# A hybrid decoder layer on one core: a third place for turned tiles in w_up, their steps in line there, and w_down's groups of seven at other steps

## The chip, the core and the metric

The kernel runs on one core of a Trainium2 chip. The time is that of one execution in device microseconds; smaller is better. A core has TensorE (PE, with a weight load PEld ahead of each matmul), VectorE (DVE), ScalarE (ACT), GpSimd (POOL) and SyncE (SP). Here SP issues nearly all loads of weights and the transposing DMAs, and POOL issues DMAs that add two weight blocks.

## The reference

One layer on 256 tokens of 2048 features in float32:

```python
u = rmsnorm(h, norm_mix_pre)
h = h + rmsnorm(hybrid_mixer(u, ...) , norm_mix_post)      # w_in, SSD and attention heads, w_out
hdn = relu(rmsnorm(h, norm_mlp_pre) @ w_up)                # 2048 -> 8192
h = h + rmsnorm((hdn * hdn) @ w_down, norm_mlp_post)       # 8192 -> 2048
```

The change touches the last two lines alone.

## The kernel before

**Exact products.** Matmuls are made of halves: every float32 operand is split into a high part (`hi`, a rounding copy on ACT, L150) and a low part (`lo`, the difference on DVE, L151), and a product is three matmuls, hi·hi, hi·lo and lo·hi (L382 to L384). A matmul of 128 x 128 by 512 columns is the unit in which TensorE's work is counted.

**Units.** `unit` (L502) computes a pair of column blocks of 512 for both token tiles of 128. It walks over `order`, steps of 256 rows of the weight (two blocks of 128). A plain step calls `row_tiles` for both column blocks: 24 matmuls, two loads of 512 KB, two splits of 128 x 1024. A step of the set `by_seven` calls `seven` (L437), which forms the same 2 x 2 x 2 block products from seven block products instead of eight: 21 matmuls. For that it needs sums of the activations' blocks (`sums_of_acts`, L419: four DVE additions and a split, made one step ahead and kept for the next unit) and sums of the weights' blocks: three additions on DVE (L275), and splits of `raw_a`, `e`, `raw_b` and `t4` (three of 128 x 1024, one of 128 x 512). One block of the second load is the sum of two blocks, which POOL forms in DRAM by two DMAs (`next_pair`, L293, up to four sevens ahead of its use); SP then loads it as the source `pair`. `combine_new` (L473) makes the accumulators' sums after a unit's last seven.

**Lookahead.** Split weights lie in five buffers of each kind (`BUFS`), raw weights in four and a few more that a stage has to spare (`room["raw"]`). ACT and DVE therefore run ahead of TensorE by little more than a step.

**The MLP.** w_up and w_down are taken in two halves (`hf`) of 4096 hidden features. In the first half w_up has three units (blocks 2 and 3, 4 and 5, 6 and 7), in the second half four. Each has seven steps in `order` with sevens at steps 1, 3, 4 and 6 (`UP_SEVENS`), and a last plain step of its own. Then w_down has two units in each half, for the columns 0 to 1023 and 1024 to 2047, with orders of 14 and 12 or 13 steps. The unit of columns 0 to 1023, here "the first w_down pair", is the one whose order changes.

**Turned tiles.** Each w_up unit leaves four tiles of 128 tokens x 512 hidden features in the queue `beside`. w_down needs them transposed. `turned` (L1517) does it in two parts. The first (the *pump*, `pump_beside`) is relu and square on ACT, a copy on ACT that sorts the 16-bit halves of the words into `halves`, and a transposing DMA on SP (L1525) back into the tile. The second (the *landing*, `land_beside`) is a copy on ACT that puts the 16-bit halves together, and the split into `sh` and `sl` or the like. `halves` is one of the places in `room["halves"]`: two in w_up, four in w_down of the first half, two in the second.

**When they stand.** `TURNS` and `LANDS` (L58, L59) name the steps at which `unit` pumps one tile and lands one; the first tuple of each is for orders of seven steps, the second for longer ones. A pump stands ahead of its step's weights, a landing behind them. w_up's tiles are pumped and landed in the next unit; those of a half's last w_up unit in the first w_down pair.

**Order on the engines.** A scheduler places instructions by priority, and what is at high priority keeps the program's order. `in_line` adds an order written out by hand: an instruction in it comes behind the last split or addition of the line on ACT and DVE (`line`). Weights' splits and additions are in line. A turned tile's copies and split are in line in w_down (`exact`), except for the landing at step 0; in w_up they have ordinary priority, only not before the newest split, and the scheduler places them between the others. In both cases relu and square have ordinary priority.

**Temporaries.** `tmp` gives tiles `r` (four buffers), and `sum_tile` gives `e` (one buffer). Both already look for tiles of their own in `room["own"]` and `room["sum"]`, which no function of the kernel before sets.

Of the kernel before, what the change touches and what calls it, by code (L numbers as in the profile page):

```python
# [10 lines left out]
F32 = mybir.dt.float32  # L11
F32R = mybir.dt.float32r
BF16 = mybir.dt.bfloat16
U16 = mybir.dt.uint16
AF = mybir.ActivationFunctionType
ALU = mybir.AluOpType

P = 128
# [21 lines left out]
NB = 512  # L40
KB = 2
# [13 lines left out]
V_SEVENS = (1, 3, 5, 6)  # L55
QK_SEVENS = (1, 3, 5, 6)
PAIRS_AHEAD = 4
TURNS = ((1, 2, 4, 5), (3, 4, 8, 9))  # L58
LANDS = ((0, 3, 4, 6), (0, 6, 7, 10, 11))  # L59


def constants():
# [18 lines left out]
def hymba_layer(ctx: ExitStack, tc: tile.TileContext, x, norm_mix_pre, w_in, conv_w, conv_b, dt_bias, a_log,  # L81
                d_skip, ssm_norm_w, w_out, norm_mix_post, norm_mlp_pre, w_up, w_down, norm_mlp_post,
                consts, out):
    nc = tc.nc
    w_in, w_out, w_up, w_down = w_in[0], w_out[0], w_up[0], w_down[0]
# [61 lines left out]
    def split(hi, lo, src, scale=None):  # L147

        if scale is None:
            return (nc.scalar.activation(hi, src, AF.Copy),  # L150
                    nc.vector.tensor_tensor(lo, src, hi.bitcast(F32), op=ALU.subtract))  # L151
        return (nc.scalar.activation(hi, src, AF.Copy, scale=scale),
                nc.vector.scalar_tensor_tensor(lo, src, scale, hi.bitcast(F32), op0=ALU.mult, op1=ALU.subtract))
# [27 lines left out]
    room = {}  # L181
# [13 lines left out]
    def beside_up(raws, turn, halves=None):  # L195

        room["sums"] = [v[:, k:k + KB] for k in range(0, NK // 2, KB) for v in att[1]]
        b = hp.tile([P, NT, NB], F32, name="hb")
        room["shared"] = [[b[:, t] for t in range(NT)],
                          [hp.tile([P, NB], F32, name="wpost", bufs=2) for _ in range(NT)]]  # L200
        room["last"] = deque([room["shared"][1].pop(), hp.tile([P, NB], F32, name="junk")])
        room["shared"][1].append(room["last"][0])
        a = hp.tile([P, 3 * KB, NB], F32, name="ha")
        in_a = [a[:, k:k + KB] for k in range(0, 3 * KB, KB)]
        halves = in_a.pop(0) if halves is None else halves
        room["halves"] = deque(halves[:, i].bitcast(U16) for i in range(KB))
        room["raw"], room["turn"], room["acts"], room["chain"] = [*raws, *in_a], turn, act_u, True
        room["of_halves"], room["of_a"] = halves, in_a
        sums_of.clear()

    def beside_down():

        a = hp.tile([P, 3 * KB, 2, S], F32R, name="ha")
        room["sums"] = [a[:, k] for k in range(3 * KB)]
        room["raw"], room["turn"], room["acts"] = [mws[2]], 0, part
        room["halves"] = deque(mws[0][:, t, c0:c0 + NB].bitcast(U16) for t in range(NT) for c0 in (0, NB))
        room["then"] = [(4, halves_beside_down), (2, more_beside_down), (0, all_beside_down)]
        sums_of.clear()
# [60 lines left out]
    w_z, w_v, w_ups, w_downs = w_in[:, COL_Z:], w_in[:, COL_V:], [w_up[:, hf * 4096:] for hf in range(2)], [w_down, w_down[4096:]]  # L279
# [8 lines left out]
    def plan(name, src, n, order, by_seven):  # L288

        orders[name, n] = order_of(order, by_seven)  # L290
        pairs.extend((src, blocks_of(n), k) for k in order if k in by_seven)
# [55 lines left out]

    beside, flying = deque(), deque()

    def pump_beside(exact=False):  # L350

        if not beside:
            return
        work = beside.popleft()
        room["exact"] = exact
        with tc.issue_after(newest["act"].ins):
            next(work)
        flying.append(work)

    def land_beside(exact=False):  # L360

        room["exact"] = exact
        if flying:
            with tc.issue_after(newest["act"].ins):
                next(flying.popleft(), None)
        if "then" in room and len(beside) + len(flying) <= room["then"][0][0]:
            room["then"].pop(0)[1]()
            if not room["then"]:
                room.pop("then")
# [123 lines left out]
    for hf in range(2):  # L493
        for n in range(0 if hf else 2, 8, 2):
            plan(("up", hf), w_ups[hf], n, range(7), UP_SEVENS)
        if hf == 0:
            plan(("down", 0), w_down, 0, (0, 1, 4, 2, 3, 6, 5, 7, 9, 8, 10, 12, 11, 13), (4, 6, 9, 10, 11, 13))
            plan(("down", 0), w_down, 2, (0, 4, 1, 6, 2, 9, 11, 3, 13, 5, 10, 7, 8), (4, 6, 9, 11, 13, 10, 8))
    plan(("down", 1), w_downs[1], 0, (0, 1, 3, 2, 4, 6, 5, 7, 8, 10, 9, 12, 11, 13), (3, 6, 8, 9, 11, 13))
    plan(("down", 1), w_downs[1], 2, (0, 1, 3, 2, 6, 8, 4, 11, 13, 5, 9, 12), (3, 6, 8, 11, 13, 9, 12))  # L500

    def unit(src, n, order, last, acc, more, combine, lag=0, at_end=(None, None), first=True, ending=None,  # L502
             ready=None, halves=None):


        cols = blocks_of(n)
        sevens = [k for k, by_seven in order if by_seven]
        for i, (k, by_seven) in enumerate(order):
            if i in TURNS[len(order) > 7]:
                pump_beside(len(order) > 7)  # L510
            if i + 1 < len(order) and order[i + 1][1]:
                sums_of_acts(order[i + 1][0])
            if by_seven:
                if k == sevens[0]:
                    drain()
                    if ready:
                        ready()
                seven(src, *cols, k, acc, more, k == sevens[0], k == sevens[-1])
            else:
                for b in range(2):  # L520
                    row_tiles(src, cols[b], [k], acc[b::2], room["acts"], first and i == 0, False,
                              fetch=fetch_next)
            if i in LANDS[len(order) > 7]:
                land_beside(len(order) > 7 and i > 0)
            if k == sevens[-1]:
                combine(more)
        for b in range(2):
            if b and ending:
                ended.append(ending(cols[b], last, acc))
            else:  # L530
                row_tiles(src, cols[b], last, acc[b::2], room["acts"], False, True, lag if b else 0, at_end[b],
                          fetch=fetch_last if b else fetch_next, halves=halves if b else None)
# [973 lines left out]
            beside.append(turned(t, 4 * fb, r))  # L1506
        return at_end

    def perhaps_in_line(dst, src):

        if not room["exact"]:
            nc.scalar.activation(dst, src, AF.Copy)
            return
        with tc.high_priority(offset=AHEAD), in_line():
            newest["act"] = line["act"] = nc.scalar.activation(dst, src, AF.Copy)

    def turned(t, k, r):  # L1517
        room["halves"].rotate(1)
        halves = room["halves"][0]
        ts = slice(t * P, (t + 1) * P)  # L1520
        words = r.bitcast(U16)
        nc.scalar.activation(r, r, AF.Relu, scale=rmlp[:, t:t + 1])
        nc.scalar.activation(r, r, AF.Square)
        perhaps_in_line(halves.rearrange("p (h n) -> p h n", h=2), words.rearrange("p (n h) -> p h n", h=2))
        nc.sync.dma_start_transpose(words.rearrange("p (n s) -> p n s", s=P), halves)  # L1525
        yield
        perhaps_in_line(halves.rearrange("p (n h) -> p h n", h=2), words.rearrange("p (h n) -> p h n", h=2))
        d_h, d_l, i = part(k)
        whole = halves.bitcast(F32).rearrange("p (f s) -> p f s", f=4)
        if not room["exact"]:  # L1530
            split(d_h[:, i:i + 4, ts], d_l[:, i:i + 4, ts], whole)
            return
        with tc.high_priority(offset=AHEAD):
            split_in_line(d_h[:, i:i + 4, ts], d_l[:, i:i + 4, ts], whole)

# [16 lines left out]
    for hf in range(2):  # L1552
        if hf:
            beside_up([], 0)
        for fb in range(0 if hf else 2, 8, 2):
            room["last"].rotate(1)
            room["shared"][1][1] = room["last"][0]
            unit(w_ups[hf], fb, orders[("up", hf), fb], (7,), acc, more,
                 lambda x: combine_new(room["shared"], x), 0, (up_end(fb, 0), up_end(fb + 1, 1)))
            acc, more = more, acc  # L1560
        if hf == 0:
            beside_down()
            unit(w_down, 0, orders[("down", 0), 0], (14, 15), acc, more,
                 lambda x: combine_new(in_mw(0), x), 0, (onto(0), onto(1)))
            room["raw"], room["turn"] = [new_mw(2)], 0
            room["sums"] += room["sums"][:4]
            unit(w_down, 2, orders[("down", 0), 2], (12, 14, 15), more, acc,
                 onto_new_mw, 0, (onto(2), onto(3)))
# [65 lines left out]
```

## Time and profile before

| | |
|---|---|
| time, median of 3 runs | 1447.81 us (1447.37 to 1448.24) |
| time of the profiled execution | 1447.99 us |
| its span | 1445.9 us |
| TensorE clock granted | 0.999 |
| first w_down pair, first half | about 936 to 1009 us |
| last w_up unit | about 1226 to 1268 us |
| first w_down pair, second half | about 1268 to 1343 us |
| bytes moved by DMA | 340.30 MB, mean 235 GB/s |

A row of an engine's timeline has start and duration in us, engine, line, operation, tiles and shape, and in brackets how long the engine sat idle just before and who ended that. Rows of a pipelined engine overlap: the distance of two starts is then the better measure of what an instruction takes. The view of windows gives for each stretch the busy time and the number of instructions of each engine. Matmuls' ends are modelled, so a TensorE that counts as busy need not be at its full rate.

### The profile page before, as it was taken

Reading aid. Unit: us, or ns where it says so; the run is one execution under the profiler, and the core shown is the slowest. Engines: PE = TensorE matmul, PEld = TensorE weight load, DVE = VectorE, ACT = ScalarE, POOL = GpSimd, SP = SyncE. Lnnn points to the kernel's source line nnn. Section 1 sums busy time; section 2 is a strip of 40 time slices with the busy share of each in tenths; the row PEclk is TensorE's granted clock in tenths of the full one; section 3 lists DMA queues with packets and bytes.
Section 4 is the critical chain, followed back from the end, with each engine's and each line's share of the span. In section 5 each row is a group of like instructions: output and inputs, shape, how many; then the busy total and the mean of one; then the engine's idle time right before and its main releaser. Section 6 shows DMA issues by size and latency. Waiting matters only on the chain.

```text
span 1445.9 us, 20240 instructions
## 1 busy us (share of the span) xinstructions
PE 1432.9 (99%) x6930; PEld 1202.2 (83%) x6930; DVE 1298.9 (90%) x1881; ACT 1002.0 (69%) x1407; POOL 162.3 (11%) x244
## 2 busy tenths in 40 slices
PE   9999999999999999999999999999999999999998
PEld 8888888888888888888888888887888888787886
DVE  7788888988999778689988999999999999999998
ACT  7577669666666666556667579877565799978664
POOL 0201110131111000011100011001111011101000
PEclk9999999999999999999999999999999999999999
DMA  8977656766888648588876799798898899899964
GB/s 266 280 212 226 190 173 181 244 175 195 221 253 254 192 124 256 167 267 259 269 238 219 197 355 278 203 256 232 265 260 264 249 272 292 240 288 258 293 207 146
DMA packets 201926, 340.30 MB, mean 235 GB/s; under 512 B 45616, under 2 KB 48544, under 8 KB 201824
## 3 DMA queue, kind: packets, MB, share of 16 engines
q1 hardware_dynamic: 174304, 279.72, 61.9%
q0 software_dynamic: 19648, 45.63, 15.6%
q10 hardware_dynamic: 7872, 13.68, 2.9%
q8 instruction: 54, 0.88, 0.2%
q14 instruction: 48, 0.39, 0.1%
HBM read 327.39 MB, written 49.84 MB: 261 GB/s over the span
## 4 chain that ended last, share of the span: by engine, by line
PE 60%; DVE 8%; ACT 4%; issue 3%; DMA 3%; ACTq 0%; DVEq 0%
PE acc L384 8%; PE acc L383 8%; PE acc L382 8%; PE acc L470 5%; PE acc L471 5%; PE acc L469 5%; PE acc L540 4%; DVE lo L151 4%; ACT hi L150 2%; PE acc L543 2%; PE ps L384 2%; PE ps L383 2%; PE ps L382 2%; PE ps L471 2%; PE ps L470 2%
## 5 line engine op out<-in xcount | busy, mean ns | idle before, releaser
L151 DVE TENSOR_TENSOR lo<-raw,hi 128x1024 fp32r<-128x1024 f32 (+1 forms) x390 | 474.1, 1220 | 78.0 <-ACT hi L150 76.2
L150 ACT ACTIVATE hi<-raw 128x1024 fp32r<-128x1024 f32 (+1 forms) x390 | 405.9, 1048 | 172.8 <-PE acc L384 50.1
L540 PE MATMUL acc<-ua,hi 128*128 128x512 f32 x520 | 141.2, 400 | 0.0
L150 ACT ACTIVATE hi<-e 128x1024 fp32r<-128x1024 f32 x66 | 69.9, 1060 | 65.4 <-DVE e L275 56.6
L540 PEld LDWEIGHTS acc<-ua,hi 128*128 128x128 f32 x520 | 91.2, 189 | 14.0
L382 PE MATMUL acc<-hi,ua 128*128 128x512 f32 x228 | 90.1, 395 | 0.0
L383 PE MATMUL acc<-lo,ua 128*128 128x512 f32 x228 | 89.2, 391 | 0.0
L384 PE MATMUL acc<-hi,ua 128*128 128x512 f32 x228 | 89.0, 390 | 0.0
L382 PE MATMUL acc<-hi,sh 128*128 128x512 f32 x220 | 86.4, 393 | 0.0
L384 PE MATMUL acc<-hi,sl 128*128 128x512 f32 x220 | 85.7, 389 | 0.0
L383 PE MATMUL acc<-lo,sh 128*128 128x512 f32 x220 | 85.6, 389 | 0.0
L543 PEld LDWEIGHTS acc<-ua,lo 128*128 128x128 f32 x520 | 76.5, 189 | 8.9
L151 DVE TENSOR_TENSOR lo<-e,hi 128x1024 fp32r<-128x1024 f32 x66 | 80.7, 1222 | 1.4 <-ACT hi L150 1.3
L543 PE MATMUL acc<-ua,lo 128*128 128x256 f32 x520 | 78.8, 281 | 0.0
L470 PE MATMUL acc<-lo,ah 128*128 128x512 f32 x180 | 70.4, 391 | 1.0 <-DVE lo L151 1.0
L471 PE MATMUL acc<-hi,al 128*128 128x512 f32 x180 | 70.1, 389 | 0.0
L469 PE MATMUL acc<-hi,ah 128*128 128x512 f32 x180 | 70.0, 389 | 0.0
L151 DVE TENSOR_TENSOR lo<-ha,hi 128x1024 fp32r<-128x1024 f32 x48 | 58.5, 1223 | 3.4 <-ACT hi L150 3.2
L540 PE MATMUL acc<-uc,hi 128*128 128x512 f32 x208 | 61.4, 405 | 0.0
L150 ACT ACTIVATE hi<-ha 128x1024 fp32r<-128x1024 f32 x48 | 50.2, 1050 | 8.6 <-PE acc L384 5.1
L470 PE MATMUL acc<-lo,ua 128*128 128x512 f32 x137 | 53.5, 391 | 0.4 <-DVE lo L151 0.3
L469 PE MATMUL acc<-hi,ua 128*128 128x512 f32 x137 | 53.5, 390 | 0.0
(577 smaller groups left out, 3725.0 us busy)
## 6 DMA issues: line engine op xcount, KB each, us to landing
raw<-in_w_in_dram SPq DMA_DIRECT2D x154, 512.0 KB, 4.5
raw<-in_w_down_dram SPq DMA_DIRECT2D x69, 512.0 KB, 6.2
raw<-in_w_up_dram SPq DMA_DIRECT2D x65, 512.0 KB, 5.3
raw<-in_w_out_dram SPq DMA_DIRECT2D x38, 512.0 KB, 5.2
raw<-pair SPq DMA_DIRECT2D x60, 256.0 KB, 4.6
pair<-in_w_up_dram POOLq DMA_DIRECT2D x56, 256.0 KB, 6.3
pair<-in_w_down_dram POOLq DMA_DIRECT2D x52, 256.0 KB, 6.0
ha<-in_w_up_dram SPq DMA_DIRECT2D x25, 512.0 KB, 6.2
```

The source lines that it names most:

```text
L150: return (nc.scalar.activation(hi, src, AF.Copy), nc.vector.tensor_tensor(lo, src, hi.bitcast(F32), op=ALU.subtract))
L151: nc.vector.tensor_tensor(lo, src, hi.bitcast(F32), op=ALU.subtract))
L382: nc.tensor.matmul(dst[:, cs], a_h[:, r, ts], hi[:, j, cs], start=begin and j == 0, stop=False)
L383: nc.tensor.matmul(dst[:, cs], a_h[:, r, ts], lo[:, j, cs], start=False, stop=False)
L384: product[t] = nc.tensor.matmul(dst[:, cs], a_l[:, r, ts], hi[:, j, cs], start=False, stop=end and j == KB - 1)
L469: nc.tensor.matmul(dst, a_h, hi[:, j], start=own and first, stop=False)
L470: nc.tensor.matmul(dst, a_h, lo[:, j], start=False, stop=False)
L471: nc.tensor.matmul(dst, a_l, hi[:, j], start=False, stop=own and last)
L540: nc.tensor.matmul(acc[f], hi[:, j, f * P:(f + 1) * P], u(k0 + j), start=k0 + j == 0, stop=False, skip_group_check=True)
L543: nc.tensor.matmul(acc[f][:, 0], lo[:, j, f * P:(f + 1) * P], u(k0 + j)[:, 0], start=False, stop=k0 + j == NK - 1, skip_group_check=True)
```

## The change

The pumps of w_up's units move by a step or so and its landings with them, so that up to three tiles are under way at once; one of the four temporaries `r` becomes the third place of `halves` while w_up runs, and `tmp` and `sum_tile` use tiles taken once for the whole of w_up. All turned tiles' copies and splits stand in line at high priority, in w_up and at the landing of step 0 too. In the first w_down pair of both halves the order of steps is another, with the same sevens.

```diff
-TURNS = ((1, 2, 4, 5), (3, 4, 8, 9))
-LANDS = ((0, 3, 4, 6), (0, 6, 7, 10, 11))
+TURNS = ((2, 3, 4, 6), (3, 4, 8, 9))
+LANDS = ((0, 4, 5, 6), (0, 6, 7, 10, 11))
...
+    def places_of_up():
+
+        own = [hp.tile([P, NB], F32, name="r", bufs=4) for _ in range(4)]
+        room["halves"].append(own.pop().bitcast(U16))
+        room["own"], room["sum"] = deque(own), hp.tile([P, KB, NB], F32, name="e")
+
+    def beside_up_no_more():
+
+        del room["own"], room["sum"]
+        room["halves"] = deque(room["of_halves"][:, i].bitcast(U16) for i in range(KB))
...
-    def pump_beside(exact=False):
+    def pump_beside():
...
-        room["exact"] = exact
...
-    def land_beside(exact=False):
-
-        room["exact"] = exact
+    def land_beside():
+
...
-            plan(("down", 0), w_down, 0, (0, 1, 4, 2, 3, 6, 5, 7, 9, 8, 10, 12, 11, 13), (4, 6, 9, 10, 11, 13))
+            plan(("down", 0), w_down, 0, (0, 1, 4, 2, 6, 3, 5, 9, 7, 10, 8, 11, 12, 13), (4, 6, 9, 10, 11, 13))
...
-    plan(("down", 1), w_downs[1], 0, (0, 1, 3, 2, 4, 6, 5, 7, 8, 10, 9, 12, 11, 13), (3, 6, 8, 9, 11, 13))
+    plan(("down", 1), w_downs[1], 0, (0, 1, 3, 2, 6, 4, 5, 8, 7, 9, 10, 11, 12, 13), (3, 6, 8, 9, 11, 13))
...
-                pump_beside(len(order) > 7)
+                pump_beside()
...
-                land_beside(len(order) > 7 and i > 0)
+                land_beside()
...
-    def perhaps_in_line(dst, src):
-
-        if not room["exact"]:
-            nc.scalar.activation(dst, src, AF.Copy)
-            return
+    def copy_in_line(dst, src):
+
         with tc.high_priority(offset=AHEAD), in_line():
             newest["act"] = line["act"] = nc.scalar.activation(dst, src, AF.Copy)
...
-        perhaps_in_line(halves.rearrange("p (h n) -> p h n", h=2), words.rearrange("p (n h) -> p h n", h=2))
+        copy_in_line(halves.rearrange("p (h n) -> p h n", h=2), words.rearrange("p (n h) -> p h n", h=2))
         nc.sync.dma_start_transpose(words.rearrange("p (n s) -> p n s", s=P), halves)
         yield
-        perhaps_in_line(halves.rearrange("p (n h) -> p h n", h=2), words.rearrange("p (h n) -> p h n", h=2))
+        copy_in_line(halves.rearrange("p (n h) -> p h n", h=2), words.rearrange("p (h n) -> p h n", h=2))
         d_h, d_l, i = part(k)
         whole = halves.bitcast(F32).rearrange("p (f s) -> p f s", f=4)
-        if not room["exact"]:
-            split(d_h[:, i:i + 4, ts], d_l[:, i:i + 4, ts], whole)
-            return
         with tc.high_priority(offset=AHEAD):
             split_in_line(d_h[:, i:i + 4, ts], d_l[:, i:i + 4, ts], whole)
...
+        places_of_up()
         for fb in range(0 if hf else 2, 8, 2):
...
+        beside_up_no_more()
         if hf == 0:
             beside_down()
```

## The prediction, made before the changed kernel ran

> **What bounds the kernel now.** I read the head of the profile page first, then the busy time by stage, then the rows of single engines where the stages show a loss.
>
> ```profile
> span 1445.9 us, 20240 instructions
> ...
> PE 1432.9 (99%) x6930; PEld 1202.2 (83%) x6930; DVE 1298.9 (90%) x1881; ACT 1002.0 (69%) x1407; POOL 162.3 (11%) x244
> ```
>
> ```profile
> 820.00:936.00 116.00, 116.00 (x513) 96.10 (x512) 110.25 (x131) 98.77 (x117) 14.82 (x22) 1.00 0.96 277
> 936.00:1010.00 74.00, 72.49 (x318) 59.04 (x317) 70.44 (x97) 55.85 (x66) 7.67 (x12) 1.00 0.92 238
> 1010.00:1225.00 215.00, 215.00 (x950) 177.76 (x949) 202.44 (x247) 152.45 (x172) 26.28 (x39) 1.00 0.92 266
> 1225.00:1268.00 43.00, 42.24 (x185) 34.24 (x184) 40.89 (x51) 35.90 (x44) 4.88 (x7) 1.00 0.88 241
> 1268.00:1344.00 76.00, 73.87 (x318) 58.81 (x318) 70.71 (x97) 58.70 (x69) 8.12 (x12) 1.00 1.01 287
> 1344.00:1436.00 92.00, 92.00 (x407) 76.11 (x406) 88.59 (x117) 52.40 (x65) 2.72 (x4) 1.00 0.63 203
> ```
>
> The columns are window and length, then busy time and instructions of PE, weight load, DVE, ACT, POOL. TensorE is the bound almost everywhere. Where it never waits, 950 matmuls take 215.00 us, 0.2263 us each; 513 in 116.00 and 407 in 92.00 give 0.2261. So I count matmuls instead of busy time. The first w_down pair of the first half (936 to 1010) has 318, worth 71.96 of its 74.00 us: **2.0 us lost**. The last w_up pair (1225 to 1268) has 185, worth 41.87 of 43.00: **1.1 lost**. The first w_down pair of the second half (1268 to 1344) has 318 in 76.00: **4.0 lost**. The change can win at most these 7.1 us, because nothing else that it touches loses TensorE time.
>
> Two adjacent matmul starts lie 0.23 us apart, though a row's duration is 0.39. [...]
>
> Who makes TensorE wait in these stages?
>
> ```profile
> 1262.71 0.50 PE L383 MATMUL acc<-lo,uc 128*128 128x512 f32 x1 [0.76 <-DVE lo L151]
> ```
>
> ```profile
> 1258.41 1.37 ACT L1512 ACTIVATE ha<-wpost 128x1024 uint16<-128x1024 uint16 x1 [1.49 <-DMA wpost<-ha]
> 1259.82 0.63 ACT L150 ACTIVATE ah<-ha 128x512 fp32r<-128x512 f32 x1
> 1260.36 1.04 ACT L150 ACTIVATE hi<-raw 128x1024 fp32r<-128x1024 f32 x1
> ```
>
> At the end of w_up it is a landing of a turned tile. Its copy sat on ACT until the transposing DMA had landed (1.49 us idle), copy and split followed, and only at 1260.36 came the high half of the last weights; their low half on DVE is what TensorE waited for at 1262.71.
>
> ```profile
> 967.66 0.69 DVE L151 TENSOR_TENSOR al<-mw,ah 128x512 fp32r<-128x512 f32 x1 [0.70 <-ACT ah L150]
> ...
> 971.49 0.69 DVE L151 TENSOR_TENSOR al<-mw,ah 128x512 fp32r<-128x512 f32 x1 [0.52 <-ACT ah L150]
> ...
> 974.81 1.23 DVE L151 TENSOR_TENSOR lo<-raw,hi 128x1024 fp32r<-128x1024 f32 x1 [1.30 <-ACT hi L150]
> ...
> 978.82 0.69 DVE L151 TENSOR_TENSOR lo<-r,hi 128x512 fp32r<-128x512 f32 x1
> ...
> 1008.35 0.69 DVE L151 TENSOR_TENSOR lo<-r,hi 128x512 fp32r<-128x512 f32 x1
> ```
>
> ```profile
> 1287.34 1.23 DVE L151 TENSOR_TENSOR lo<-uc,hi 128x1024 fp32r<-128x1024 f32 x1 [0.92 <-ACT hi L150]
> ...
> 1301.94 0.69 DVE L151 TENSOR_TENSOR al<-ha,ah 128x512 fp32r<-128x512 f32 x1 [1.11 <-ACT ah L150]
> ...
> 1305.77 0.69 DVE L151 TENSOR_TENSOR al<-ha,ah 128x512 fp32r<-128x512 f32 x1 [0.52 <-ACT ah L150]
> ...
> 1309.09 1.22 DVE L151 TENSOR_TENSOR lo<-uc,hi 128x1024 fp32r<-128x1024 f32 x1 [1.30 <-ACT hi L150]
> ...
> 1313.11 0.69 DVE L151 TENSOR_TENSOR lo<-r,hi 128x512 fp32r<-128x512 f32 x1
> ...
> 1342.63 0.68 DVE L151 TENSOR_TENSOR lo<-r,hi 128x512 fp32r<-128x512 f32 x1
> ```
>
> In both w_down pairs DVE is the second bound, and it first wastes time, then lacks it. It idles 0.70 + 0.52 + 1.30 = 2.5 us in the first half and 0.92 + 1.11 + 0.52 + 1.30 = 3.85 in the second, each time behind a copy of a turned tile on ACT that stands beside a step without a seven. Later, from the last low half of the third seven (978.82, 1313.11) to that of the sixth (1008.35, 1342.63), it runs for 29.5 us with no such wait. TensorE's work there is three sevens of 21 matmuls and two plain steps of 24, 111 x 0.2263 = 25.1 us. DVE falls 4.4 us behind; what lead it had is short of that by the 2.0 and 4.0 us lost.
>
> **The change part by part.** No matmul, split or byte is added or taken away. What moves is order, one place, and lines on ACT.
>
> *The sevens of w_down.* The first w_down pair of each half has them at steps 2, 5, 8, 10, 12, 13 by the order lists; after the change at 2, 4, 7, 9, 11, 13. Each brings its weight loads, its pair load and its sums along. Three loads on SP replace two at that step, and the pairs on POOL are still fetched four sevens ahead, so neither queue gets more to do.
>
> ```profile
> 949.21 2.36 DVE L151 TENSOR_TENSOR lo<-raw,hi 128x1024 fp32r<-128x1024 f32 x2
> ```
>
> From the third to the sixth seven there are then three plain steps instead of two. A plain step costs DVE 2.3 us (949.21, two low halves) and gives TensorE 24 x 0.2263 = 5.4. So DVE needs 29.5 + 2.3 = 31.8 against TensorE's 25.1 + 5.4 = 30.5: 1.3 behind instead of 4.4. The plain step is taken from the front, where DVE wastes its spare time. DVE's sum to step 13 stays what it was, so the end of step 13 comes earlier only by the idle time that goes. The turned tiles keep their steps in w_down: pumps at 3, 4, 8, 9, landings at 0, 6, 7, 10, 11. Before, landings 6 and 7 and pump 8 came with plain steps 6 and 7; now step 7 is a seven, which leaves DVE a queue of work while ACT copies. The landings at 10 and 11 that stood by sevens in the trace of before have no idle DVE row behind them. I leave 1.0 us of idle in each half (one landing of 0.70 between two plain steps, and 0.3 for the rest): 2.5 - 1.0 = **1.5 us won** of 2.0 in the first half, 3.85 - 1.0 = **2.9 won** of 4.0 in the second. Bounds: 0 (the idle comes back elsewhere) to 2.0 and 4.0. A loss is excluded as long as the sevens' pairs are in time.
>
> *The third place and the steps of w_up.* Pumps go from steps 1, 2, 4, 5 to 2, 3, 4, 6, landings from 0, 3, 4, 6 to 0, 4, 5, 6. Three tiles are then in flight after step 4's pump, which two places could not hold; one of the four temporaries becomes the third.
>
> ```profile
> 1229.44 1.06 ACT L1512 ACTIVATE ha<-hb 128x1024 uint16<-128x1024 uint16 x1 [3.04 <-DVE sl L151]
> ```
>
> ```profile
> DMA to landing us min/median/max: 2.7/5.8/9.7
> ```
>
> The 3.04 us that ACT waited for a place at 1229.44 go; TensorE lost nothing there. Three temporaries suffice: a seven takes one and its sums two, and sums are made only in the second half's first w_up unit, which has no tile to turn. A tile now has three steps from pump to landing, about 15 us (two sevens and a plain step, 4.75 + 4.75 + 5.4); the transposing line's DMAs took up to 9.7 us. So a copy in line need not wait for its DMA as the one at 1258.41 did, the third tile's first copy is no longer put off, and the **1.1 us** lost at the end of w_up go; I count 1.0, with 0 as the other end.
>
> *The price: steps in line.* What is behind a copy on ACT must now wait for it.
>
> ```profile
> 945.76 0.71 ACT L1522 ACTIVATE hb<-hb,rmlp 128x512 f32<-128x512 f32 x1
> ...
> 948.13 1.99 ACT L150 ACTIVATE hi<-raw 128x1024 fp32r<-128x1024 f32 x2
> ...
> 965.61 1.36 ACT L1515 ACTIVATE mw<-hb 128x1024 uint16<-128x1024 uint16 x1
> ...
> 967.53 1.04 ACT L150 ACTIVATE hi<-mw 128x1024 fp32r<-128x1024 f32 x1
> ...
> 1235.33 1.05 ACT L150 ACTIVATE hi<-raw 128x1024 fp32r<-128x1024 f32 x1
> ...
> 1245.34 1.04 ACT L150 ACTIVATE hi<-e 128x1024 fp32r<-128x1024 f32 x1
> ...
> 1247.75 1.04 ACT L150 ACTIVATE hi<-ha 128x1024 fp32r<-128x1024 f32 x1
> ```
>
> ```profile
> 1241.64 0.39 PE L469 MATMUL ps<-hi,ua 128*128 128x512 f32 x1
> ```
>
> In line (w_down, before) a pump takes ACT 948.13 - 945.76 = 2.4 us and a landing 967.53 - 965.61 = 1.9; a plain step's two high halves take 1.9, a seven's 0.95 + (1247.75 - 1245.34) = 3.4. From the pump of step 3 to the last high half of step 6, ACT has three pumps, two landings, three sevens and a plain step: 7.2 + 3.8 + 10.2 + 1.9 = 23.1 us. TensorE, from step 3 to the last product of step 6, has 4.75 + 4.75 + 5.43 + 4.1 = 19.0. ACT must be 4.1 us ahead at step 3, some 5.5 with DVE's low halves behind it. It was: step 3's first high half began at 1235.33 and TensorE's step 3 at 1241.64, 6.3 us. It is just enough, and I charge **0.7 us** over the five w_up units with turned tiles: hf 0 has two, hf 1 three. The bounds are 0 and 5 x (0.52 + 1.30) = 9.1, the idle that copies in line cost DVE in one w_down pair.
>
> ACT takes its instructions in order here: at 1258.41 nothing passed the waiting copy. [...]
>
> *The sum.* 1.5 + 2.9 + 1.0 - 0.7 = 4.7 us. After 1344 TensorE runs without a gap (407 matmuls in 92.00), and between 1010 and 1225 likewise, so a gain in a stage reaches the end. The profiled execution took 1447.99 us, 2.1 above its span and 0.18 above the median of 1447.81. 1447.99 - 4.7 - 0.18 = **1443.1 us**.
>
> **Rivals.** *ACT becomes the bound in w_up* (slower). If ACT's lead at step 3 is under 5.5 us, which is 0.8 less than the row shows, step 6's high halves come late in each of five units. At 0.52 + 1.30 us each that is 9.1 us, against 4.4 won in w_down: 1447.8 + 4.7 = 1452.5. For it speak ACT's 98.77 busy of 116.00 us and DVE's 110.25 in w_up; against it, that pumps come later in the unit, so less is asked early. *The stall only moves* (no change). DVE's work to step 13 is the same; with copies in line everywhere, half of the idle may return at other steps and w_up's end win nothing: (1.5 + 2.9) / 2 - 0.7 = 1.5, so 1446.3. *The whole ceiling* (faster still): 7.1 us, 1440.7. *It does not take*: relu and square of a pump keep their low priority, and the scheduler could lay them as before; then 1447.8, part of no change.
>
> **How the numbers follow.** About 0.2% (2.9 us) is what a measurement of this kernel can tell from no change. Forecast (gains from 2.9 to 6 us) 0.44, whole ceiling 0.11, stall moves or change does not take 0.26, ACT bound 0.19. So faster 0.55, same 0.26, slower 0.19. The range runs from the ceiling, 1440.4, to 1451.0, which takes in all of "same" and the mild end of the slower rival. The forecast's own range is 1441.8 to 1444.9.
>
> **What would show it.** Right: 318 matmuls of the two w_down pairs fit into about 72.5 and 73.1 us; DVE's idle behind ACT at steps 6 to 8 is gone; no copy on ACT waits for its DMA at the end of w_up; w_up from 820 to 936 keeps 513 matmuls in 116.00 us. Wrong: matmul counts in w_up fall below 0.2263 us each (ACT bound), or DVE's idle in w_down stays near 2.5 and 3.85 us (stall moved), or a load from DRAM or pair ends DVE's waits.

## The result and the profile after

| | before | after |
|---|---|---|
| time, median of 4 runs each on one chip | 1447.59 us | 1470.82 us (1466.65 to 1472.65) |
| ratio | | 1.0164, 95% interval 1.0152 to 1.0176 |
| time of the profiled execution | 1447.99 us | 1466.65 us |

The change makes the kernel 23 us slower. The forecast was 1443.1 us and its range ended at 1451.0. The profiled execution of after is the shortest of its four; its span is 19.0 us longer than that of before, and those 19.0 us can be followed in the trace.

The head of the page of after:

```profile
span 1464.9 us, 20234 instructions
...
PE 1445.3 (99%) x6930; PEld 1200.0 (82%) x6930; DVE 1300.1 (89%) x1881; ACT 1006.4 (69%) x1407; POOL 162.7 (11%) x244
```

The engines have hardly more to do: DVE has 1300.1 us of work against 1298.9, ACT 1006.4 against 1002.0, and the number of matmuls is the same. So the time went into waiting. Where, the view of windows tells; the borders are set so that in after a window holds w_up or w_down alone, to within a few us (from 1010 to 1140 both kernels have 575 matmuls and lose nothing). First after:

```profile
820.00:944.00 124.00, 121.61 (x518) 95.33 (x517) 113.01 (x135) 101.03 (x117) 14.95 (x22) 1.00 0.88 255
944.00:1010.00 66.00, 65.74 (x289) 53.76 (x288) 63.27 (x87) 51.24 (x60) 7.92 (x12) 1.00 0.94 260
...
1140.00:1280.00 140.00, 136.28 (x571) 104.19 (x570) 126.78 (x154) 117.98 (x139) 16.32 (x24) 1.00 0.94 248
1280.00:1344.00 64.00, 59.49 (x252) 47.60 (x251) 53.34 (x71) 46.74 (x53) 6.79 (x10) 0.97 0.99 268
1344.00:1436.00 92.00, 91.64 (x403) 75.17 (x402) 90.45 (x114) 60.36 (x71) 4.08 (x6) 1.00 0.70 228
```

The same windows before:

```profile
820.00:944.00 124.00, 124.00 (x549) 102.70 (x547) 118.25 (x143) 101.40 (x120) 15.72 (x23) 1.00 0.94 270
944.00:1010.00 66.00, 64.49 (x282) 52.44 (x281) 62.45 (x85) 53.22 (x63) 6.78 (x10) 1.00 0.95 246
...
1140.00:1280.00 140.00, 139.24 (x613) 114.56 (x612) 133.55 (x164) 119.90 (x143) 16.25 (x24) 1.00 0.96 262
1280.00:1344.00 64.00, 61.87 (x266) 48.88 (x265) 59.25 (x81) 51.02 (x61) 7.58 (x11) 1.00 1.02 294
```

A window's length less its matmuls at 0.2263 us gives TensorE's loss:

| window | stage | lost before | lost after |
|---|---|---|---|
| 820 to 944 | w_up, first half | 0 | 6.8 |
| 944 to 1010 | first w_down pair, first half | 2.2 | 0.6 |
| 1140 to 1280 | w_up, second half (before: and the start of w_down) | 1.3 | 10.8 |
| 1280 to 1344 | first w_down pair, second half | 3.8 | 7.0 |
| 1344 to 1436 | w_down after it | 0 | 0.8 |
| sum | | 7.3 | 26.0 |

The difference, 18.7 us, is nearly the whole of the 19.0. In the first half w_down gained 1.6 us, which is what the prediction counted (1.5). In the second half it lost 3.2. And **w_up lost 16.3 us**, where 0.7 had been charged. DVE is *less* busy than before in w_up, 113.01 us of 124 against 118.25 and 126.78 of 140 against 133.55, and ACT no busier, 101.03 against 101.40 and 117.98 against 119.90.

What happens in w_up. Rows of ACT, then of DVE, then of TensorE in after:

```profile
880.88 0.71 ACT L1528 ACTIVATE junk<-junk,rmlp 128x512 f32<-128x512 f32 x1
...
882.29 1.06 ACT L1521 ACTIVATE r<-junk 128x1024 uint16<-128x1024 uint16 x1
883.25 1.04 ACT L150 ACTIVATE hi<-raw 128x1024 fp32r<-128x1024 f32 x1
```

```profile
884.33 1.23 DVE L151 TENSOR_TENSOR lo<-raw,hi 128x1024 fp32r<-128x1024 f32 x1 [1.30 <-ACT hi L150]
```

```profile
884.75 0.39 PE L478 MATMUL acc<-hi,uc 128*128 128x512 f32 x1
885.61 0.50 PE L479 MATMUL acc<-lo,uc 128*128 128x512 f32 x1 [0.47 <-DVE lo L151]
```

A pump (relu, square, copy) takes ACT from 880.88 to 883.25, 2.4 us, ahead of the next seven's first high half. DVE has nothing left to do and idles 1.30 us; TensorE, which needs the low half, starts its second matmul of that seven 0.86 us after the first instead of 0.23. Waits of this kind return in every w_up unit that has turned tiles. By the view of waits DVE waits 9.5 and 10.5 us for ACT's high halves in the two w_up windows (before 5.5 and 3.3), and ACT waits 15.2 and 18.2 us for `e`, the first of a seven's sums (before 9.2 and 6.7). TensorE loses its 16 us in many small steps: its waits there are none longer than 0.5 us, 4.4 us in sum for high halves of ACT and 1.2 for low halves of DVE, and the rest are matmuls that start farther apart than 0.2263 us.

Where ACT's time went shows in two more rows of ACT and one of TensorE:

```profile
856.42 1.06 ACT L150 ACTIVATE hi<-e 128x1024 fp32r<-128x1024 f32 x1 [6.24 <-DVE e L286]
...
1251.71 1.04 ACT L150 ACTIVATE hi<-raw 128x1024 fp32r<-128x1024 f32 x1
```

```profile
1254.61 0.39 PE L478 MATMUL ps<-hi,ua 128*128 128x512 f32 x1
```

In a unit's first seven ACT now waits 6.0 to 6.2 us for `e`. Before, the unit's first pump floated into that wait. Now the pumps of steps 2 and 3 stand ahead of those steps' high halves, and ACT's lead on TensorE at step 3 is 1254.61 - 1251.71 = **2.9 us** in the last w_up unit, where the prediction read 6.3 us in the kernel before. It is 2.9 us in three of the five units and 4.2 in the first of each half; before it was 6.3 to 6.6.

What happens in the second half's w_down pair. Rows of SP, ACT and TensorE in after:

```profile
1272.46 11.89 SPq L164 DMA_DIRECT2D raw<-in_w_down_dram  x5
...
1303.91 2.61 SPq L164 DMA_DIRECT2D uc<-in_w_down_dram  x2
1306.57 1.58 SPq L1531 DMA_TRANSPOSE hb<-ha  x1
```

```profile
1289.33 1.06 ACT L150 ACTIVATE hi<-raw 128x1024 fp32r<-128x1024 f32 x1 [3.14 <-DMA raw<-in_w_down_dram]
...
1295.28 1.06 ACT L1521 ACTIVATE ha<-hb 128x1024 uint16<-128x1024 uint16 x1
...
1316.65 1.37 ACT L1521 ACTIVATE ha<-hb 128x1024 uint16<-128x1024 uint16 x1 [6.97 <-DMA hb<-ha]
```

```profile
1319.97 0.39 PE L478 MATMUL acc<-hi,ah 128*128 128x512 f32 x1
1322.73 0.50 PE L479 MATMUL acc<-lo,ah 128*128 128x512 f32 x1 [2.37 <-DVE lo L151]
...
1325.06 0.63 PE L480 MATMUL acc<-hi,ua 128*128 128x512 f32 x1
1325.48 0.63 PE L478 MATMUL acc<-hi,ua 128*128 128x512 f32 x1
```

SP issues five weight loads in a row and needs 11.89 us for them; the weights then come late to ACT (3.14 us at 1289.33). The first pump's copy is done at 1296.34, but SP, which issues loads in between, issues the transposing DMA only at 1306.57, 10.2 us later, and it lands another 10.1 us later. The landing of that tile is in line on ACT and holds ACT for 6.97 us (1316.65), and TensorE waits 2.37 us.

The late issue alone is not new: before, the same tile's DMA was issued 9.1 us after its copy and landed 8.7 us after that. Two things differ. The way from copy to landing takes 20.3 us instead of 17.8, and ACT comes to the landing 13.3 us after the copy, where before it came after 17.5 and waited 0.29 us.

### The profile page after: what moved, and what is told of

Same layout as the page of the kernel before. It is cut to its first block, busy times and chain, and to the rows that moved or that the text cites. A ratio compares the mean times of both kernels' runs of the same rounds, so it can differ in the third digit from the quotient of the medians.

```text
span 1464.9 us, 20234 instructions
## 1 busy us (share of the span) xinstructions
PE 1445.3 (99%) x6930; PEld 1200.0 (82%) x6930; DVE 1300.1 (89%) x1881; ACT 1006.4 (69%) x1407; POOL 162.7 (11%) x244
## 3 DMA queue, kind: packets, MB, share of 16 engines
q0 software_dynamic: 19648, 45.63, 15.2%
## 4 chain that ended last, share of the span: by engine, by line
PE 57%; ACT 7%; DVE 7%; issue 3%; DMA 3%; ACTq 0%; SPq 0%; DVEq 0%
PE acc L392 8%; PE acc L393 8%; PE acc L391 8%; PE acc L478 5%; PE acc L479 5%; PE acc L480 5%; ACT hi L150 4%; PE acc L549 4%; DVE lo L151 3%; PE acc L552 2%; PE ps L392 2%; PE ps L393 2%; PE ps L391 2%; PE ps L479 2%; PE ps L480 2%
## 5 line engine op out<-in xcount | busy, mean ns | idle before, releaser
L150 ACT ACTIVATE hi<-ha 128x1024 fp32r<-128x1024 f32 x48 | 49.9, 1051 | 10.1 <-issue 3.1
```

What stands on the lines that cost most here:

```text
L150: return (nc.scalar.activation(hi, src, AF.Copy), nc.vector.tensor_tensor(lo, src, hi.bitcast(F32), op=ALU.subtract))
```

## The experiments

All times are medians. Each experiment was compared with the kernel before on the same chip, and its ratio is to that; experiments that ran on different chips are compared by their ratios. Experiments 1 to 4 take the change apart; 5 to 8 ask what it is about copies in line that costs so much; 9 to 14 test the answer and what remained.

**1. The new order alone** (`e1_orders`): the kernel before with the two new order lists.

> The kernel before with the new order of steps in the first w_down pair of both halves alone. The prediction's own step: 4.4 us won, ratio 0.997 (about 1443.4 us). Rival (the landing that waited 6.97 us for its transpose in the changed kernel belongs to this order, since SP issues the transpose behind more loads of weights): nothing won in the second half or up to 8 us lost there, 1446 to 1454 us.

1443.23 against 1446.44 us, ratio 0.9982 (0.9972 to 0.9992): 3.2 us by the medians, 2.6 by the ratio. The windows of this run (before had 318, 185 and 318 matmuls in them):

```profile
936.00:1010.00 74.00, 73.78 (x324) 60.01 (x323) 71.79 (x99) 57.73 (x67) 8.14 (x12) 1.00 0.91 245
...
1225.00:1268.00 43.00, 43.00 (x190) 35.31 (x190) 42.48 (x52) 36.14 (x44) 4.87 (x7) 1.00 0.98 247
1268.00:1344.00 76.00, 75.27 (x331) 61.65 (x330) 73.17 (x101) 62.68 (x72) 8.14 (x12) 1.00 0.99 291
```

Losses are 0.7, 0 and 1.1 us instead of 2.0, 1.1 and 4.0. TensorE wins what was forecast (1.3 and 2.9, forecast 1.5 and 2.9). Of DVE's waits for ACT, which the prediction wanted to bring down to 1.0 us in each half, 2.0 and 2.7 us are left, from 3.2 and 4.4 (view of waits). The loss at the end of w_up, which the third place and the new steps were to remove, is gone too, without either.

**2. The change with the old order** (`e2_old_orders`).

> The changed kernel with the old order of steps in w_down: new steps of pumps and landings, third place, copies in line. If the loss of 17 us that the changed kernel's TensorE shows before 1285 us is w_up's alone, it stays: 1462 to 1467 us. If the order of w_down brings the rest, this kernel lacks the 8 us stall at 1320 us and is some 6 to 9 us faster than the changed one. If the two only work badly together, it is within 3 us of the kernel before.

1465.61, ratio 1.0130 (1.0114 to 1.0145). So some 19 of the 23 us are lost in the turned tiles' part, and inside the change the new order costs some 5 us (1.0164 against 1.0130) where alone it wins 3. The landing of step 6 in the second half's w_down pair, in rows of ACT:

```profile
1315.36 1.37 ACT L1521 ACTIVATE ha<-hb 128x1024 uint16<-128x1024 uint16 x1 [1.86 <-DMA hb<-ha]
```

With the old order it holds ACT for 1.86 us; in after it was 6.97. Here too SP takes 11.87 us for five loads in a row, and the tile lands 19.3 us after its copy; but ACT comes to the landing 17.5 us after the copy, with the new order after 13.3. In experiment 1 ACT comes after 13.4 us as well, and the tile has just landed, after 13.2.

**3. In line alone** (`e3_in_line`): old steps, two places, old order.

```diff
-                pump_beside(len(order) > 7)
+                pump_beside(True)
...
-                land_beside(len(order) > 7 and i > 0)
+                land_beside(True)
```

> The kernel before with turned tiles' copies and splits in line in w_up too; old steps of pumps and landings, two places, old order in w_down. Theory that being in line is the cause (each copy holds ACT ahead of a high half): 10 to 17 us slower, 1458 to 1465 us. Theory that the new steps are the cause (two pumps and three landings crowd from step 4 on): no more than 3 us slower.

1473.77, ratio 1.0190 (1.0175 to 1.0205): 27 us lost by these two arguments alone, at least as much as by the whole change (23 us).

**4. New steps and third place, floating** (`e4_steps_third`): `TURNS`, `LANDS`, `places_of_up` and `beside_up_no_more` as in the change, copies in w_up at ordinary priority, old order.

> The kernel before with the new steps of pumps and landings and the third place with its own temporaries, but copies not in line in w_up and the old order in w_down. Theory that being in line is the cause: within 3 us of before, 1445 to 1451 us. Theory that the new steps crowd the unit's second half: 5 to 15 us slower, since the scheduler can spread the copies but not move their work forward.

1449.02, ratio 1.0019 (1.0009 to 1.0028). No gain of 1.0 us but a small loss. This run differs from experiment 2 only in that the copies float in w_up and at the landing of step 0: 1.0019 against 1.0130, on the same chip. So being in line there costs 16 us in the change itself. With the copies floating, ACT waits up to 6.2 us for `e` in a unit's first seven here too, but its lead at step 3 is 6.6 to 7.3 us. In one place a pump of step 6 floats back so far that its tile's landing, at step 0 of the next unit, comes 5.3 us after the copy and must wait for its DMA; a little later TensorE waits 0.76 us (1235.13):

```profile
1225.49 1.04 ACT L1523 ACTIVATE ha<-wpost 128x1024 uint16<-128x1024 uint16 x1
1230.83 1.38 ACT L1523 ACTIVATE ha<-wpost 128x1024 uint16<-128x1024 uint16 x1 [4.30 <-DMA wpost<-ha]
```

**5. Only pumps in line** (`e5_pump_in_line`) and **6. only landings in line** (`e6_land_in_line`): the one or the other half of the diff of experiment 3.

> The kernel before with only the pumps' copies in line in w_up; landings there as before, old steps, two places, old order in w_down. With both in line the run was 27 us slower than before. Theory of the burst (a pump's relu, square and copy hold 2.4 us of ACT ahead of a step's high halves): 15 to 27 us slower. Theory of the tie (a landing's low half stands on DVE ahead of the weights' additions, so DVE waits for ACT's copy and ACT then for DVE's additions): under 8 us slower.

> The kernel before with only the landings' copies and splits in line in w_up and at step 0; pumps there as before, old steps, two places, old order in w_down. Theory of the tie: 15 to 27 us slower. Theory of the burst: under 10 us slower. If neither alone is slow and only both together are, each is under 8 us slower.

Pumps: 1471.84, ratio 1.0178 (1.0163 to 1.0193), 26 us. Landings: 1452.11, ratio 1.0044 (1.0027 to 1.0060), 6 us. It is the pump. Its window in the first half's w_up (before: 513 matmuls, DVE 110.25 and ACT 98.77 us busy), and rows of ACT and of DVE:

```profile
820.00:936.00 116.00, 110.43 (x474) 87.63 (x473) 102.61 (x121) 90.58 (x108) 14.36 (x21) 1.00 0.97 271
```

```profile
858.68 0.71 ACT L1522 ACTIVATE hb<-hb,rmlp 128x512 f32<-128x512 f32 x1
...
860.08 1.06 ACT L1515 ACTIVATE mw<-hb 128x1024 uint16<-128x1024 uint16 x1
861.05 1.99 ACT L150 ACTIVATE hi<-raw 128x1024 fp32r<-128x1024 f32 x2
862.95 1.04 ACT L150 ACTIVATE hi<-mw 128x1024 fp32r<-128x1024 f32 x1
865.91 1.07 ACT L150 ACTIVATE hi<-e 128x1024 fp32r<-128x1024 f32 x1 [1.92 <-DVE e L275]
```

```profile
862.13 2.36 DVE L151 TENSOR_TENSOR lo<-raw,hi 128x1024 fp32r<-128x1024 f32 x2 [1.36 <-ACT hi L150]
864.40 0.69 DVE L275 TENSOR_TENSOR e<-mw 128x512 f32<-128x512 f32 x1
```

Here both engines idle, one after the other. From 858.68 to 861.05 ACT works on the pump; DVE runs dry and loses 1.36 us (862.13). DVE is then late with the low halves ahead of the seven's first sum `e` (864.40), and ACT, which needs `e` for its next high half, loses 1.92 us (865.91). A seven has such a hole on ACT by itself, since `hi<-e` must wait for additions on DVE. The kernel before often fills it with a floating copy. Rows of ACT, before:

```profile
1171.10 1.06 ACT L1512 ACTIVATE ha<-junk 128x1024 uint16<-128x1024 uint16 x1
1172.06 1.04 ACT L150 ACTIVATE hi<-e 128x1024 fp32r<-128x1024 f32 x1
```

Between the first high half of a seven and `hi<-e`, a turned tile's copy stands in 15 of the 20 sevens of these units before, and in none in this run and in after.

In line ahead of the step, the copy takes ACT's time when DVE needs ACT, and leaves it free when it has to wait for DVE. That is a theory so far; experiments 7 to 9 and 12 test it.

**7. In line, without relu and square** (`e7_no_relu_square`): experiment 3 without the two instructions of the first part of `turned`.

> The kernel with pumps and landings in line in w_up (old steps, two places, old order in w_down) without the relu and square of turned tiles, so the computation leaves out the activation of these tiles: a pump holds ACT 1.1 us instead of 2.4. Theory of the burst: each pump costs DVE 1.3 us less idle time, four pumps in five units, so 15 to 25 us of the 27 come back, 1449 to 1459 us. Theory of the tie: under 8 us come back, 1465 us or more.

1462.20, ratio 1.0111 (1.0096 to 1.0126): some 11 of 27 us back, between the ranges of the two theories. They stand ahead of the copy and count in its price, but they take work off ACT as well, so the run can't say how much of the 11 is their place.

**8. In line, a landing's low half outside the line** (`e8_low_half_free`): experiment 3 with the difference of a landing at ordinary priority on DVE.

> The kernel with pumps and landings in line in w_up (old steps, two places, old order in w_down), but a landing's low half on DVE has ordinary priority and stands outside the line, in w_up and in w_down. Theory of the tie: DVE no longer waits for the landing's copies ahead of the additions, 10 to 20 us of the 27 come back. Theory of the burst: under 8 us come back; DVE's waits of 1.3 to 2.5 us behind a pump stay.

1476.55, ratio 1.0211 (1.0189 to 1.0233). Nothing comes back, so the landing's tie between ACT and DVE is not what costs.

**9. Pumps in the seven's hole** (`e9_pump_in_hole`): in line as in experiment 5, but pumped inside `seven` ahead of `hi<-e`, two places, old order.

```diff
-TURNS = ((1, 2, 4, 5), (3, 4, 8, 9))
+TURNS = ((1, 3, 4, 6), (3, 4, 8, 9))
...
             add_in_line(t4, e[:, 1], raw_a[:, 1])
+            if pump:
+                pump_beside(True)
             hl_e = parts()
```

> The kernel before with w_up's pumps in line, but inside a seven: behind its first high half and third addition, ahead of the high half of the sums, where ACT waits 1.5 to 2.4 us for DVE's additions anyway; pumps at steps 1, 3, 4, 6, all sevens. Landings, places and w_down's order as before. Theory of the hole (in line the copies stand ahead of a step's weights and leave ACT's waits inside the sevens empty): 0 to 8 us slower than before, against 26 with the pumps in line ahead of the steps. Theory of the burst alone (2.4 us of ACT in a row delay DVE wherever they stand): still 15 us or more slower. Theory that being in line itself is dear (relu waits for the add of the unit before and everything waits behind it): still 15 us or more.

1459.18, ratio 1.0092 (1.0078 to 1.0106): the loss falls from 26 to 13 us by another place in line (inside the seven, and at steps 1, 3, 4 and 6 instead of 1, 2, 4 and 5). That lies between the ranges expected. What is left shows in a row of ACT:

```profile
883.07 1.06 ACT L1518 ACTIVATE mw<-junk 128x1024 uint16<-128x1024 uint16 x1 [1.77 <-DVE sl L151]
```

The copy waits for a place of `halves`, which is free when the landing's low half `sl` has been made. In line, everything behind it on ACT waits as well.

**10. The third place alone, floating** (`e10_third_place`).

> The kernel before with the third place and its own temporaries alone; old steps, copies not in line in w_up, old order in w_down. With the new steps too it was 2.6 us slower than before. If the place (three temporaries, one sum tile) costs that, 1448 to 1450 us; if the new steps do, within 1.5 us of before.

1445.43, ratio 0.9993 (0.9984 to 1.0003): no difference that can be told from noise. Its trace has 190 matmuls from 1225 to 1268, as that of experiment 1, so the loss at the end of w_up is gone here too; a gain of 1.0 us is too small for the times to show. The small loss of experiment 4 is thus the new steps' own.

**11. The whole change, floating in w_up** (`e11_change_floating`): experiment 4 with the new order.

> The changed kernel without being in line in w_up and at step 0: new steps, third place and new order in w_down, copies there at ordinary priority. If the stall of 8 us near 1320 us (a landing waits 6.97 us for its transpose) only follows from w_up's delay, the new order is worth here what it was alone, 3 to 5 us: 1443 to 1446 us. If it comes from the new steps and order together, 1450 us or more.

1448.69, ratio 1.0015 (1.0004 to 1.0026). If the order had been worth here what it was alone, 1443 to 1446 us would have come out; it wasn't. The window of the second half's w_down pair in this run:

```profile
1268.00:1344.00 76.00, 73.56 (x319) 59.20 (x318) 73.25 (x102) 60.80 (x72) 8.13 (x12) 1.00 0.91 276
```

It has 319 matmuls, about as few as before (318) and 5 more than experiment 4 (314), where the order alone has 331. Why the new steps take the order's gain away here wasn't settled.

**12. Pumps in the hole, with the third place** (`e12_hole_third`) and **13. with the new order too** (`e13_hole_third_order`): experiment 9 with `places_of_up` and `beside_up_no_more`; then the two order lists as well.

> Pumps in line inside the sevens (steps 1, 3, 4, 6) as in the run that was 12.8 us slower than before, with the third place and its own temporaries added; landings and w_down's order as before. In that run ACT's copy then waited 1.1 to 2.1 us per pump for DVE's low half of an older landing, which frees the place. Theory of the place: these waits go and 8 to 13 us come back, 1446 to 1451 us. Theory that 2.4 us in a row inside a seven delay DVE anyway: under 5 us come back, 1454 us or more.

> The same with the new order of steps in w_down. If w_up's end is on time the order is worth 3 us as it was alone, so 3 us less than without it; if w_up still ends late, the order loses 2 to 5 us as in the changed kernel.

Experiment 12: 1446.72 against 1447.12, ratio 1.0003 (0.9994 to 1.0013). With the pumps in line in w_up nothing is lost any more. (The landings float there, unlike in the change; in line they cost 6 us by experiment 6.) A pump's copy stands ahead of `hi<-e` in all 20 sevens. Experiment 13: 1443.40, ratio 0.9973 (0.9963 to 0.9983), faster than both kernels; its interval overlaps with that of experiment 1, and the two can't be told apart. The window of w_up and rows of ACT in experiment 12:

```profile
820.00:936.00 116.00, 115.69 (x511) 95.48 (x510) 110.34 (x133) 98.89 (x117) 14.63 (x22) 1.00 0.94 272
```

```profile
863.50 0.71 ACT L1536 ACTIVATE hb<-hb,rmlp 128x512 f32<-128x512 f32 x1
...
864.90 1.06 ACT L1529 ACTIVATE mw<-hb 128x1024 uint16<-128x1024 uint16 x1
865.87 1.05 ACT L150 ACTIVATE hi<-e 128x1024 fp32r<-128x1024 f32 x1
```

The same pump as in experiment 5 now fills the wait for `e` (which is ready at 864.82, so the copy runs 1.1 us over), and `hi<-e` has no idle time ahead of it. There are 511 matmuls in the window, with DVE and ACT as busy as before (110.34 and 98.89 us).

**14. The change with w_down's landings a step later** (`e14_land_later`).

```diff
-LANDS = ((0, 4, 5, 6), (0, 6, 7, 10, 11))
+LANDS = ((0, 4, 5, 6), (0, 7, 8, 10, 11))
```

> The changed kernel with the first two landings of the first w_down pair one step later, at steps 7 and 8 instead of 6 and 7. The landing that waited 6.97 us for its transpose then comes some 5 us of work later. Theory that this wait is what the new order loses: 3 to 8 us faster than the changed kernel, 1463 to 1468 us. Theory that the loads of w_down are late themselves and the wait only shows it: within 2 us of the changed kernel's 1470.8 us.

1466.01, ratio 1.0126 (1.0104 to 1.0149), 5 us less loss than the change. This bears out that in after the landing at step 6 comes too early for its transpose. It does not repair the order's part fully; rows of ACT:

```profile
1320.48 1.36 ACT L1521 ACTIVATE ha<-hb 128x1024 uint16<-128x1024 uint16 x1
...
1330.70 1.36 ACT L1521 ACTIVATE ha<-hb 128x1024 uint16<-128x1024 uint16 x1 [3.55 <-DMA hb<-ha]
```

The first tile's copy no longer waits, the second's still does, 3.55 us.

## Why the prediction was wrong

**The step that failed is the price of the steps in line**, 0.7 us with bounds of 0 and 9.1. In the change w_up lost 16.3 us, and experiments 2 and 4 put 16 us on being in line there; in the kernel before, being in line alone costs 27 (experiment 3). The working counted ACT's instructions against TensorE's time, asked for a lead of 5.5 us at step 3, and took 6.3 from a row of before. In after the lead is 2.9 us (three units) or 4.2 (two). So the row could not be carried over: in line, the pumps stand ahead of the high halves of steps 2 and 3, and the wait of 6.2 us in the first seven, where the first pump had floated, stays empty.

The count also treats ACT as an engine with a sum of work to finish. But ACT and DVE hand each other halves: a low half needs its high half, and `hi<-e` needs DVE's additions. What matters is what each has *next*. A copy at the wrong place idles DVE, DVE's delay then idles ACT, and each engine is below its load before (experiment 5: DVE 102.61, ACT 90.58 of 116 us). The ledger had no term for this.

**The upper bound was no bound.** It took 0.52 + 1.30 us a unit from a w_down pair in which ACT was busy 55.85 of 74.00 us and so free for 25% of the time. In w_up ACT was busy 98.77 of 116.00 us and free for 15% (DVE for 5% in both). The prediction quoted these numbers of w_up itself, for the rival, and didn't let them widen the bound. Measured over five units, 16.3 us are 3.3 a unit.

**The rival "ACT becomes the bound in w_up"** had the right place, sign and condition, at 0.19: a lead under 5.5 us at step 3 is what after shows. Step 6 comes late as it said (its first high half starts at 883.25, its matmuls at 884.75, 1.5 us apart; before 6.6), but other steps do too, and ACT is less busy than before, not more. Its price was too low: it gave 1452.5. By the prediction's own test, fewer matmuls than 513 from 820 to 936, the reader could have told it at once; after has 490 there.

**The third place and the new steps** were to win 1.0 us at the end of w_up. In the traces that loss goes with the third place alone (experiment 10) and with the new order alone (experiment 1), and the times can't tell 1.0 us from noise. The new steps cost nearly 4 us against the third place (experiment 4, 1.0019 against 0.9993): the prediction counted on three steps or 15 us from pump to landing, and a floating pump came 5.3 us ahead of its landing. In after itself no copy of a turned tile waits for a place or a DMA in w_up, as forecast. The prediction also read at 1229.44 that TensorE loses nothing to a wait for a place. That holds for floating copies. In line it doesn't: with the pumps inside the sevens, the third place is worth some 13 us (1.0092 to 1.0003, experiments 9 and 12). The prediction took a cost of the old arrangement over into the new one without asking what had hidden it.

**The new order**: alone it won 1.3 and 2.9 us in the trace, and 2.6 to 3.2 in the time, so the size was right. The mechanism held in part: DVE's waits for ACT fell from 3.2 to 2.0 and from 4.4 to 2.7 us, less far than to the 1.0 us forecast, so that 2.9 came out exactly is partly luck. In the change the first half kept its gain (1.6), the second did not. There the prediction had excluded a loss as long as the pairs were in time, and had written that neither queue gets more to do. That holds for the number of DMAs but not for when a tile is back: after the late w_up the way from copy to landing takes 19 to 20 us with either order (experiment 2: 19.3, after: 20.3), and the new order brings ACT to the landing after 13.3 us instead of 17.5. Why the loads and transposes then take longer was not shown. The prediction had read at 1258.41 that nothing on ACT passed a copy that waited 1.49 us for its DMA, and so had named the mechanism; its sum charged nothing for such a wait, and in after it was 6.97 us on ACT.

**The ceiling of 7.1 us** and the matmul count as a measure held: experiment 1 won 5.3 of the 7.1 in three windows.

**Left open**: how the 11 us of experiment 7 divide; why the new steps take the order's gain away in experiment 11; and how much of the loss in line is the lower clock of the last section.

## What to carry to other kernels

Where two engines feed each other in a fixed order, don't price an added instruction by its engine's sum of work: go along the rows and ask which instruction of the *other* engine waits behind it, and put it where its engine has to wait for the other anyway. Work that floats shows no cost because the scheduler lays it into such holes; before fixing its place, look at which holes it filled, and at every wait (a place, a DMA) that was harmless only because nothing stood behind it. A lead that a row of before shows belongs to the order of before. Take bounds for a cost from a stretch that is as full as the one it goes to.

## What the chip showed

**After some short waits TensorE ran at a lower clock for about 3 us.** In after, following the wait of 2.37 us shown above, the matmuls at 1325.06 and 1325.48 start 0.42 us apart instead of 0.23, and this goes on to about 1327.2. The view of windows there:

```profile
1324.00:1328.00 4.00, 4.00 (x11) 2.84 (x10) 3.74 (x6) 2.60 (x4) 0.81 (x1) 0.57 1.03 293
```

The granted clock (the column ahead of the last two) is 0.57, and 11 matmuls ran in 4.00 us where 17.7 would have fitted. In experiment 3 the same followed a wait of 1.72 us (881.24): from 883 to 887 the granted clock is 0.57, and matmuls start 0.43 us apart from 883.76 to 886.33. In experiment 9 it followed one of 1.67 us (1255.76): 0.43 us apart from 1257.84 to 1260.40. It did not follow every such wait: in experiment 5 TensorE waits 1.99 us at 881.55, and afterwards the matmuls start 0.23 us apart, at a granted clock of 1.00 from 884 to 888; in experiment 9 it waits 1.55 us at 1295.99, and from 1297.51 they start 0.23 us apart. What decides was not shown. So a wait can come with a loss beyond its own length, in after 6.7 matmuls or 1.5 us at 0.2263. As an estimate for whole runs: the mean clock of after is 0.997 against 0.999 before, and 0.002 of 1465 us are about 2.9 us. Its other three runs had 0.995 to 0.996 and took 4 to 6 us longer than the profiled one, so a good part of their excess may be this. All four runs of experiment 2 had 0.999; of the some 5 us that the new order costs inside the change, 0.003 x 1470 = 4.4 may be clock. Experiment 14 ran from 1467.25 us at 0.997 to 1462.21 at 1.000. Experiments 3, 5 and 8 had mean clocks of 0.994 to 0.996, so by the same estimate some 5 to 7 of their 26 to 30 us may be clock; experiment 2 lost its 19 us at 0.999.

**SP's own time.** A transposing DMA often holds SP for 1.23 us (up to 3.43 before), but here also for 6.99; the five loads took 11.89. Rows of SP in after:

```profile
1269.60 1.23 SPq L1531 DMA_TRANSPOSE junk<-ha  x1
...
1312.94 6.99 SPq L1531 DMA_TRANSPOSE hb<-ha  x1
```

From issue to landing the transposes took up to 9.7 us before and up to 12.4 after:

```profile
DMA to landing us min/median/max: 2.7/7.1/12.4
```
